# Split weight halves stored with the columns of two k-tiles interleaved

## The chip, the cores and the metric

The kernel runs on one core of one Trainium2 chip. The metric is the device time of one execution, in microseconds. The kernel before takes 2815.72 us, the median of three runs (2814.26 to 2816.58).

## The reference

Two transformer blocks in a row, on one sequence of 256 tokens with 2048 features, all in float32. The first has an adaptive modulation (a matrix of 2048 x 12288 on one vector), a projection `w_in`, stick-breaking attention in 8 heads, sparse attention with an indexer in 8 heads, two output projections with gates, and a feed-forward part of 5632 with a causal convolution of width 3. The second has a projection, 8 heads of attention with a forget gate, 8 heads of a three-branch sparse attention, and a SwiGLU of 5632. Cut to the products that matter here:

```python
def first_block(x, ...):
    mod = silu(c) @ w_ada + b_ada
    h = modulate(rms_norm(x, g_mix), sh1, sc1)
    z = h @ w_in                       # q, k, v, indexer and gates
    ...
    x = x + gt1 * (merged @ w_out)
    h = modulate(rms_norm(x, g_ffn), sh2, sc2)
    a = causal_dwconv(h @ w_gate, conv_w, conv_b)
    return rms_norm(x + gt2 * ((silu(a) * (h @ w_up)) @ w_down), g_final)

def second_block(x, ...):
    x = x + hybrid_mixer(rms_norm(x, attn_norm), w_in, ...)
    return x + (silu(h @ w_gate) * (h @ w_up)) @ w_down   # h = rms_norm(x, ffn_norm)
```

## The kernel before

Nearly all work is products of the activations (256 tokens) with weight matrices that are read once. They are computed to nearly float32 precision with the matmul type fp32r: each operand is written as a high half, rounded to fp32r, plus a low half, the difference; and three products are summed, high x high, high x low and low x high.

A weight tile goes through these steps. SyncE issues a DMA of 512 KB into `raw`, 128 partitions by 1024 words (`load`, L252 to L269): n k-tiles of 128 rows of the matrix, w columns of each, mostly two of 512 or four of 256. `split` (L285 to L305) makes the halves: ScalarE copies `raw` into `wh` in fp32r (L296), VectorE writes the difference into `wl` (L303; GpSimd does the first one, L301). Both have four buffers of [128, 1024] words. `view` (L292) gives both tiles the layout "p (k w)", one k-tile behind the other, so that 128 weight columns are 128 adjacent words of a partition. `products` (L381 to L384) hands out one k-tile after the other.

There are two kinds of groups. In kind "f" the weights are stationary (`mm_f`, L386 to L404): for each 128 columns of the group and each k-tile, the weight columns are loaded and the activations move past them, 256 columns for 256 tokens (258 in the first block's feed-forward part, for the convolution). A group that has `pair` uses the two activation halves at once, since they are adjacent: high weights times 512 columns (L397, or L393 for the first k-tile) and low weights times 256 (L396, or L394). This is called a pair below. The other groups do three matmuls, a triple, L399 to L401:

```python
nc.tensor.matmul(ps, hi[:, fs], xh, start=start, stop=False)
nc.tensor.matmul(ps, hi[:, fs], xl, start=False, stop=False)
nc.tensor.matmul(ps, lo[:, fs], xh, start=False, stop=stop)
```

In kind "t" (`mm_t`, L406 to L417) the activations are stationary and the weights move. These are mostly the products for v, and few. Each matmul comes with a load of its stationary operand, on a queue of its own (PEld in the profile) that runs beside the matmul ahead of it.

The activation halves live in `ring`, 13 slots of [128, 8, n] words: four k-tiles, high and low in turn, with n of 256 or 258.

The order is written out by hand. `run` (L446 to L487) goes over the items; before the matmuls of one item it issues the copies and subtractions of up to three items further on (`AHEAD`, L420; `LAG` holds the subtractions one behind the copies), and `pump_loads` (L423) keeps SyncE up to 10 loads ahead. `spent` counts matmul columns and runs the attention, norm and modulation steps in between, as small pieces on all engines. The change touches only `split` and `products`.

Of the kernel before, what the change touches and what calls it, by code (L numbers as in the profile page):

```python
# [123 lines left out]
def kernel(ctx: ExitStack, tc: tile.TileContext, t):  # L124
# [64 lines left out]
    def psm():  # L189
        return pm.tile([128, 512], F32, name="pm", tag="pm")  # L190
# [37 lines left out]
    def start(gen):  # L228
        active.append(gen)
        return gen  # L230
# [54 lines left out]
    def split(idx, g, ks, off, stage):  # L285

        it, r = items[idx], raw_of[idx]
        k0, n = ks[0], len(ks)
        if it[0] == "w":
            w = g.width  # L290
            src = r[:, k0 - it[2]:k0 - it[2] + n, off:off + w]
            view = lambda x: x[:, :n * w].rearrange("p (k w) -> p k w", w=w)  # L292
            if stage == 0:
                hi = view(wp.tile([128, 1024], F32R, name="wh", tag="wh"))
                half_of[idx, g, k0] = hi
                nc.scalar.activation(out=hi, in_=src, func=AF.Copy)  # L296
            else:
                hi, lo = half_of[idx, g, k0], view(wp.tile([128, 1024], F32R, name="wl", tag="wl"))
                if state["firsts"]:
                    state["firsts"] -= 1  # L300
                    nc.gpsimd.tensor_tensor(out=lo, in0=src, in1=hi.bitcast(F32), op=OP.subtract)  # L301
                else:
                    nc.vector.tensor_sub(out=lo, in0=src, in1=hi.bitcast(F32))  # L303
                half_of[idx, g, k0] = (hi, lo)
            return  # L305
        a = it[1]
        first = a in (0, NKG)
        if stage == 0 and k0 == 0:
            ada_acc[a] = P.get("ft", ab).tile([128, 2, 512], F32, name="adaacc", tag="adaacc", bufs=2)
            if first:  # L310
                ada_ps[a] = psm()
        for k in ks:
            side = k not in FIRST_OWN if first else k % 3 == 1 if a < 2 * NKG else k % 2 == 1
            if side != (stage == 0):
                continue
            own = FIRST_OWN.index(k) if first and not side else k // 2
            acc = ada_acc[a][:, own % 2 if first else int(side), :128 * ADA[a][1]]
            x, cs = r[:, k - it[2], :], cact[:, k:k + 1]
            if side and first:
                for j in range(ADA[a][1]):  # L320
                    nc.tensor.matmul(ada_ps[a][:, j:j + 1], x[:, 128 * j:128 * (j + 1)], cs,
                                     start=(k == 1 and j == 0), stop=False)
            elif own < (2 if first else 1):
                eng = nc.gpsimd if side else nc.vector
                eng.tensor_scalar(out=acc, in0=x, scalar1=cs, scalar2=None, op0=OP.mult)
            elif side:
                nc.scalar.activation(out=x, in_=x, func=AF.Copy, scale=cs)  # L327
                nc.gpsimd.tensor_tensor(out=acc, in0=x, in1=acc, op=OP.add)  # L328
            else:
                nc.vector.scalar_tensor_tensor(out=acc, in0=x, scalar=cs, in1=acc, op0=OP.mult, op1=OP.add)  # L330
        if stage == 1 and ks[-1] == NK - 1:
            if first:
                ada_first(a)
            else:
                fins.append(start(ada_finish(a)))
# [15 lines left out]
    def ada_first(a):  # L351
        acc, ps, w = ada_acc.pop(a), ada_ps[a], 128 * ADA[a][1]
        nc.vector.tensor_add(out=acc[:, 0, :w], in0=acc[:, 0, :w], in1=acc[:, 1, :w])
        for j in range(ADA[a][1]):
            nc.tensor.matmul(ps[:, j:j + 1], acc[:, 0, 128 * j:128 * (j + 1)], ones[:, 0:1], start=False,
                             stop=(j == ADA[a][1] - 1))
        if a == 0:
            h_scale(0)
            ada_put(NKG, ada_ps[NKG], 1)
            ada_put(0, ps, 1)  # L360

    def ada_finish(a):
        acc, w = ada_acc.pop(a), 128 * ADA[a][1]
        s = acc[:, 1, :w]
        yield
        nc.gpsimd.tensor_tensor(out=s, in0=acc[:, 0, :w], in1=s, op=OP.add)
        yield from wait(FW[a // NKG if a < 2 * NKG else 2])
        ps = psm()
        for j in range(ADA[a][1]):
            nc.tensor.matmul(ps[:, j:j + 1], s[:, 128 * j:128 * (j + 1)], ones[:, 0:1], start=True, stop=True)  # L370
        ada_put(a, ps, 1)
# [9 lines left out]
    def products(g, parts):  # L381
        ks = [(half_of[idx, g, ks[0]], kk, k) for idx, ks in parts for kk, k in enumerate(ks)]
        for j, ((hi, lo), kk, k) in enumerate(ks):
            yield hi[:, kk, :], lo[:, kk, :], *g.act(k), g.done == 0 and j == 0, g.done + j + 1 == g.nk  # L384

    def mm_f(g, parts, last):  # L386
        n = g.n
        for f in range(g.width // 128):
            fs = slice(128 * f, 128 * f + 128)
            ps = g.ps[f][:, :n]  # L390
            for hi, lo, xh, xl, both, start, stop in products(g, parts):
                if g.pair and start:
                    nc.tensor.matmul(g.ps[f], hi[:, fs], both, start=True, stop=False)  # L393
                    nc.tensor.matmul(ps, lo[:, fs], xh, start=False, stop=False)  # L394
                elif g.pair:
                    nc.tensor.matmul(ps, lo[:, fs], xh, start=False, stop=False)  # L396
                    nc.tensor.matmul(g.ps[f], hi[:, fs], both, start=False, stop=stop)  # L397
                else:
# [3 lines that stand above are left out]
                spent(3 * n)  # L402
            if last:
                g.evac(f, g.ps[f])  # L404

    def mm_t(g, parts, last):  # L406
        w = g.width
        for b in range(2):
            bs = slice(128 * b, 128 * b + 128)
            ps = g.ps[b][:, :w]  # L410
            for hi, lo, xh, xl, _, start, stop in products(g, parts):
                nc.tensor.matmul(ps, xh[:, bs], hi, start=start, stop=False)  # L412
                nc.tensor.matmul(ps, xh[:, bs], lo, start=False, stop=False)  # L413
                nc.tensor.matmul(ps, xl[:, bs], hi, start=False, stop=stop)  # L414
                spent(3 * w)
            if last:
                g.evac(b, g.ps[b])  # L417
# [12 lines left out]
    def split_stage(stage):  # L430
        idx, g, ks, off = halves[state["split"][stage]]
        if stage == 0:
            pump_loads(idx - 1)
        if items[idx][0] == "call":
            if stage == 1:
                items[idx][1]()
        elif items[idx][0] != "raw":
            split(idx, g, ks, off, stage)
        state["split"][stage] += 1
# [1349 lines left out]
```

## Time and profile before

| | |
|---|---|
| median of the runs | 2815.72 us |
| the profiled execution | 2818.41 us |
| its span | 2816.6 us |
| TensorE busy, matmuls | 2734.5 us, 97% |
| its weight loads | 2496.7 us, 89% |
| VectorE | 2007.7 us, 71% |
| ScalarE | 1424.9 us, 51% |
| GpSimd | 841.1 us, 30% |
| DMA | 590.45 MB, mean 210 GB/s |
| mean granted clock of TensorE | 0.993 |

The span is the time from the first to the last recorded instruction; the execution's own time is 1.8 us longer. PE is TensorE's matmuls, PEld its weight loads, DVE VectorE, ACT ScalarE, POOL GpSimd. Matmuls are pipelined and their ends are modelled, so that one starts while another still counts as busy; the time that one takes is read from the distance between starts, or from a count in a stretch without idle time. PEclk 1.00 means that the clock of 2.4 GHz was granted for the whole stretch. In "128*128 128x512" the first pair is the stationary tile (partitions * columns), the second the moving operand.

### The profile page before, as it was taken

Reading aid. Unit: us, or ns where it says so; the run is one execution under the profiler, and the core shown is the slowest. Engines: PE = TensorE matmul, PEld = TensorE weight load, DVE = VectorE, ACT = ScalarE, POOL = GpSimd, SP = SyncE. Lnnn points to the kernel's source line nnn. Section 1 sums busy time; section 2 is a strip of 40 time slices with the busy share of each in tenths; the row PEclk is TensorE's granted clock in tenths of the full one; section 3 lists DMA queues with packets and bytes.
Section 4 is the critical chain, followed back from the end, with each engine's and each line's share of the span. In section 5 each row is a group of like instructions: output and inputs, shape, how many; then the busy total and the mean of one; then the engine's idle time right before and its main releaser. Section 6 shows DMA issues by size and latency. Waiting matters only on the chain.

```text
span 2816.6 us, 47791 instructions
## 1 busy us (share of the span) xinstructions
PE 2734.5 (97%) x18364; PEld 2496.7 (89%) x18364; DVE 2007.7 (71%) x2804; ACT 1424.9 (51%) x2124; POOL 841.1 (30%) x710
## 2 busy tenths in 40 slices
PE   7899999899999999999999999999999999999999
PEld 7788887788988999989999888989998888888888
DVE  7999997979888986655666765676776665556654
ACT  5555564555556554434454544555554544344443
POOL 3867752545754531000110310211222220012210
PEclk9999999999999999999999999999999999999999
DMA  9777777878887876566666575544566565566654
GB/s 316 250 249 256 241 219 203 268 242 280 291 276 233 287 260 183 184 188 186 180 180 191 183 229 172 163 123 144 186 188 187 180 189 193 187 187 187 187 195 142
DMA packets 334944, 590.45 MB, mean 210 GB/s; under 512 B 21234, under 2 KB 85594, under 8 KB 334716
## 3 DMA queue, kind: packets, MB, share of 16 engines
q1 hardware_dynamic: 331236, 583.61, 65.7%
q10 hardware_dynamic: 3480, 3.79, 0.7%
q8 instruction: 144, 2.36, 0.3%
q14 instruction: 84, 0.69, 0.1%
HBM read 581.49 MB, written 5.78 MB: 209 GB/s over the span
## 4 chain that ended last, share of the span: by engine, by line
PE 76%; DVE 10%; DMA 5%; issue 4%; POOL 3%; ACT 2%; SPq 0%; DVEq 0%; ACTq 0%; POOLq 0%
PE pg L397 25%; PE pg L396 13%; PE pg L399 9%; PE pg L400 9%; PE pg L401 9%; DVE wl L303 4%; DVE adaacc L330 3%; PE pg L393 2%; DMA raw<-in_w_in 2%; PE pm L728 1%; PE pg L412 1%; ACT wh L296 1%; PE pg L414 1%; PE pg L413 1%; DMA raw<-in_w_out 1%
## 5 line engine op out<-in xcount | busy, mean ns | idle before, releaser
L303 DVE TENSOR_TENSOR wl<-raw,wh 128x1024 fp32r<-128x1024 f32 (+1 forms) x921 | 1192.1, 1306 | 658.3 <-ACT wh L296 656.1
L296 ACT ACTIVATE wh<-raw 128x1024 fp32r<-128x1024 f32 (+2 forms) x922 | 934.2, 1026 | 883.2 <-PE pg L397 497.6
L397 PE MATMUL pg<-ring,wh 128*128 128x512 f32 x3384 | 1203.9, 396 | 0.0
L396 PE MATMUL pg<-ring,wl 128*128 128x256 f32 x3384 | 957.9, 283 | 7.6 <-DVE wl L303 7.6
L399 PE MATMUL pg<-ring,wh 128*128 128x256 f32 (+1 forms) x2828 | 813.7, 288 | 9.8 <-DVE ring L1093 3.6
L401 PE MATMUL pg<-ring,wl 128*128 128x256 f32 (+1 forms) x2828 | 799.9, 283 | 13.9 <-DVE wl L303 13.8
L400 PE MATMUL pg<-ring,wh 128*128 128x256 f32 (+1 forms) x2828 | 803.7, 284 | 0.0
L397 PEld LDWEIGHTS pg<-ring,wh 128*128 128x128 f32 x3384 | 638.2, 189 | 141.4
L396 PEld LDWEIGHTS pg<-ring,wl 128*128 128x128 f32 x3384 | 638.4, 189 | 23.6 <-DVE wl L303 9.5
L401 PEld LDWEIGHTS pg<-ring,wl 128*128 128x128 f32 x2828 | 541.4, 191 | 17.8 <-DVE wl L303 17.8
L399 PEld LDWEIGHTS pg<-ring,wh 128*128 128x128 f32 x2828 | 538.2, 190 | 19.7 <-issue 7.6
L400 PEld LDWEIGHTS pg<-ring,wh 128*128 128x128 f32 x2828 | 539.5, 191 | 3.6 <-issue 2.2
L531 POOL TENSOR_TENSOR ring<-gy,ring 128x256 fp32r<-128x256 f32 x88 | 107.1, 1230 | 661.9 <-ACT ring L529 661.9
L328 POOL TENSOR_TENSOR adaacc<-raw,adaacc 128x512 f32<-128x512 f32 (+2 forms) x152 | 230.6, 1517 | 247.4 <-ACT raw L327 197.4
L330 DVE SCALAR_TENSOR_TENSOR adaacc<-raw,cact,adaacc 128x512 f32<-128x512 f32 (+2 forms) x228 | 234.2, 1031 | 3.6 <-DMA raw<-in_w_ada 2.0
L1268 POOL TENSOR_TENSOR gy<-ga,rb 128x256 f32<-128x256 f32 x44 | 53.6, 1228 | 331.1 <-ACT ga L203 331.1
L516 POOL TENSOR_TENSOR ring<-pt,ring 128x256 f32<-128x256 f32 x95 | 109.7, 1167 | 50.5 <-ACT pt L515 50.3
L327 ACT ACTIVATE raw<-raw,cact 128x512 f32<-128x512 f32 (+2 forms) x152 | 103.1, 681 | 23.3 <-DMA raw<-in_w_ada 16.9
L1163 POOL TENSOR_TENSOR ssq<-ssq,sq 128x256 f32<-128x256 f32 x60 | 63.8, 1075 | 145.3 <-ACT sq L1161 144.0
L1406 POOL TENSOR_TENSOR hm<-hm,hsq 128x512 f32<-128x512 f32 (+1 forms) x15 | 18.4, 1224 | 286.3 <-ACT hsq L203 286.3
L393 PE MATMUL pg<-ring,wh 128*128 128x512 f32 x200 | 81.9, 410 | 7.0 <-DVE ring L1169 3.6
L412 PE MATMUL pg<-wh,ring 128*128 128x512 f32 (+3 forms) x236 | 84.2, 357 | 0.0
(300 smaller groups left out, 2665.1 us busy)
## 6 DMA issues: line engine op xcount, KB each, us to landing
raw<-in_w_in SPq DMA_DIRECT2D x240, 512.0 KB, 4.6
raw<-in_w_gate SPq DMA_DIRECT2D x176, 512.0 KB, 4.2
raw<-in_w_up SPq DMA_DIRECT2D x176, 512.0 KB, 4.4
raw<-in_w_down SPq DMA_DIRECT2D x176, 512.0 KB, 4.2
raw<-in_w_ada SPq DMA_DIRECT2D x144, 512.0 KB, 5.4
raw<-in_w_out SPq DMA_DIRECT2D x64, 512.0 KB, 4.6
raw<-in_w_ada SPq DMA_DIRECT2D x64, 384.0 KB, 4.1
raw<-in_w_o_sb SPq DMA_DIRECT2D x16, 512.0 KB, 5.1
```

Source lines behind the costliest of these rows:

```text
L296: nc.scalar.activation(out=hi, in_=src, func=AF.Copy)
L303: nc.vector.tensor_sub(out=lo, in0=src, in1=hi.bitcast(F32))
L328: nc.gpsimd.tensor_tensor(out=acc, in0=x, in1=acc, op=OP.add)
L330: nc.vector.scalar_tensor_tensor(out=acc, in0=x, scalar=cs, in1=acc, op0=OP.mult, op1=OP.add)
L393: nc.tensor.matmul(g.ps[f], hi[:, fs], both, start=True, stop=False)
L396: nc.tensor.matmul(ps, lo[:, fs], xh, start=False, stop=False)
L397: nc.tensor.matmul(g.ps[f], hi[:, fs], both, start=False, stop=stop)
L399: nc.tensor.matmul(ps, hi[:, fs], xh, start=start, stop=False)
L400: nc.tensor.matmul(ps, hi[:, fs], xl, start=False, stop=False)
L401: nc.tensor.matmul(ps, lo[:, fs], xh, start=False, stop=stop)
L412: nc.tensor.matmul(ps, xh[:, bs], hi, start=start, stop=False)
L516: nc.gpsimd.tensor_tensor(out=y, in0=x, in1=y, op=OP.add)
```

## The change

In groups of kind "f" the halves are stored with the columns of two k-tiles in turn: word 2j + b of a block is column j of k-tile b of the two. A stationary tile, 128 columns of one k-tile, is then every other word of 256 adjacent ones, 8 bytes from column to column. An item with a single k-tile leaves the other places of the block empty. ScalarE's copy writes with that step, VectorE's subtraction reads the high half and writes the low half with it, and `products` hands out the tiles with it. `raw`, the DMAs, the activations, the groups of kind "t", the instructions and their order stay as they are.

```diff
@@ -290,6 +290,10 @@
             w = g.width
             src = r[:, k0 - it[2]:k0 - it[2] + n, off:off + w]
             view = lambda x: x[:, :n * w].rearrange("p (k w) -> p k w", w=w)
+            if g.kind == "f":
+
+                view = lambda x: x[:, :max(n, 2) * w].rearrange("p (a w b) -> p a b w", w=w, b=2)[:, :, :min(n, 2), :]
+                src = src.rearrange("p (a b) w -> p a b w", b=min(n, 2))
             if stage == 0:
                 hi = view(wp.tile([128, 1024], F32R, name="wh", tag="wh"))
                 half_of[idx, g, k0] = hi
@@ -381,7 +385,8 @@
     def products(g, parts):
         ks = [(half_of[idx, g, ks[0]], kk, k) for idx, ks in parts for kk, k in enumerate(ks)]
         for j, ((hi, lo), kk, k) in enumerate(ks):
-            yield hi[:, kk, :], lo[:, kk, :], *g.act(k), g.done == 0 and j == 0, g.done + j + 1 == g.nk
+            hi, lo = ((x[:, kk // 2, kk % 2, :] if g.kind == "f" else x[:, kk, :]) for x in (hi, lo))
+            yield hi, lo, *g.act(k), g.done == 0 and j == 0, g.done + j + 1 == g.nk
```

## Rows read from the trace of the kernel before

**Rows 1.** The chain of waits: shares by engine, then by line.

```profile
PE 76%; DVE 10%; DMA 5%; issue 4%; POOL 3%; ACT 2%; SPq 0%; DVEq 0%; ACTq 0%; POOLq 0%
...
PE pg L397 25%; PE pg L396 13%; PE pg L399 9%; PE pg L400 9%; PE pg L401 9%; DVE wl L303 4%; DVE adaacc L330 3%; PE pg L393 2%; DMA raw<-in_w_in 2%; PE pm L728 1%; PE pg L412 1%; ACT wh L296 1%; PE pg L414 1%; PE pg L413 1%; DMA raw<-in_w_out 1%
```

**Rows 2.** Busy time by stretch: window, us, each engine's us (x instructions), PEclk, DMA share, GB/s.

```profile
0.00:420.00 420.00, 377.94 (x2594) 349.27 (x2595) 377.63 (x534) 234.86 (x424) 270.07 (x231) 0.98 0.80 255
...
420.00:860.00 440.00, 410.40 (x2530) 360.58 (x2528) 368.98 (x510) 235.24 (x349) 232.81 (x164) 0.97 0.81 259
...
860.00:1500.00 640.00, 637.86 (x4915) 618.07 (x4915) 442.74 (x597) 323.92 (x426) 121.06 (x133) 1.00 0.67 208
...
2060.00:2816.00 756.00, 753.07 (x4307) 657.44 (x4306) 444.17 (x521) 344.05 (x455) 116.05 (x95) 1.00 0.59 184
```

**Rows 3.** By stretch, one line of matmuls each: L396, L393, L399; PE (x), PEld (x).

```profile
2104.00:2804.00 700.00, 527.81 (x1878) 353.18 (x1878) 1.00 0.59 186
...
2104.00:2804.00 700.00, 44.19 (x112) 21.08 (x112) 1.00 0.59 186
...
1300.00:1480.00 180.00, 140.98 (x500) 94.00 (x500) 1.00 0.61 180
```

**Rows 4.** Timeline of TensorE: start us, duration us, instruction; two stretches.

```profile
1740.65 0.28 PE L399 MATMUL pg<-ring,wh 128*128 128x256 f32 x1
...
1745.75 0.28 PE L399 MATMUL pg<-ring,wh 128*128 128x256 f32 x1
...
2046.61 0.29 PE L399 MATMUL pg<-ring,wh 128*128 128x256 f32 x1
...
2052.01 0.28 PE L399 MATMUL pg<-ring,wh 128*128 128x256 f32 x1
```

**Rows 5.** Weight loads by source line: duration ns min/median/max, first and last start, forms.

```profile
L763 PEld LDWEIGHTS pm<-t,relb x2: 81/82/84, 452.9 to 453.0; 32*8 32x8 f32 x2
...
L728 PEld LDWEIGHTS pm<-pcT,vcT x32: 181/182/184, 1839.6 to 1940.7; 32*128 32x128 f32 x32
...
L1500 PEld LDWEIGHTS pm<-ringw,ring x64: 134/136/156, 1669.1 to 1709.5; 128*34 128x34 f32 x64
...
L399 PEld LDWEIGHTS pg<-ring,wh x2828: 186/188/335, 30.7 to 2069.0; 128*128 128x128 f32 x189
```

**Rows 6.** Instructions ahead of and behind 860 us: L396, L393, L399; then one form.

```profile
0.00:860.00 860.00, 199.56 (x687) 131.06 (x687) 0.98 0.80 257
...
860.00:2816.00 1956.00, 758.37 (x2698) 507.31 (x2698) 1.00 0.61 189
...
0.00:860.00 860.00, 21.93 (x48) 9.89 (x48) 0.98 0.80 257
...
860.00:2816.00 1956.00, 59.99 (x152) 28.64 (x152) 1.00 0.61 189
...
0.00:860.00 860.00, 264.93 (x912) 178.06 (x912) 0.98 0.80 257
...
860.00:2816.00 1956.00, 623.09 (x2176) 409.99 (x2176) 1.00 0.61 189
...
L399 PE MATMUL pg<-ring,wh 128*128 128x258 f32 x1408 | 398.4, 283 | 1.1 <-DVE ga L1231 1.0
```

**Rows 7.** VectorE's groups by line and form: xcount, busy us, mean ns, idle before.

```profile
L303 DVE TENSOR_TENSOR wl<-raw,wh 128x1024 fp32r<-128x1024 f32 x853 | 1130.3, 1336 | 639.8 <-ACT wh L296 637.7
...
L303 DVE TENSOR_TENSOR wl<-raw,wh 128x512 fp32r<-128x512 f32 x56 | 51.6, 922 | 0.4 <-ACT wh L296 0.2
...
L1472 DVE TENSOR_SCALAR gat<-gat 128x24 f32<-128x24 f32 x2 | 0.4, 180 | 0.7 <-ACT gat L203 0.7
...
L1382 DVE TENSOR_SCALAR gcol<-vec 128x1 f32<-128x1 f32 x6 | 0.4, 138 | 0.0
```

**Rows 8.** VectorE at L303 alone, by stretch.

```profile
0.00:420.00 420.00, 179.73 (x145) 0.98 0.80 255
...
420.00:860.00 440.00, 184.04 (x124) 0.97 0.81 259
```

## Prediction

> **What bounds the kernel now.** I read the chain of waits first: three quarters of it is TensorE, and of the lines on it the five of the two matmul forms hold some 65 of 100 [rows 1]. The stretches say where: behind 860 us TensorE is idle for 2 us in 640 and for 3 in 756, while VectorE has 197 and 312 us free there; ahead of 860 us TensorE, VectorE (378 of 420, 369 of 440) and the transfers (0.80) are all nearly full, and none of them alone sets the pace [rows 2]. So up to 860 us TensorE's time counts in part, behind it in full.
>
> Then the pace, since the matmuls overlap and their own durations (283 ns for 256 columns) say little. Two stretches without an idle moment give it. From 2104 to 2804 us there are 1878 + 112 pairs (one matmul of 512 columns and one of 256): 700 us / 1990 = 351.8 ns for a pair. From 1300 to 1480 us there are 500 triples (three of 258 columns): 180 us / 500 = 360 ns [rows 3]. The granted clock in both is 1.00, the level of 2.4 GHz, at which the 768 columns of a pair take 320 ns and the 774 of a triple 322.5. So 32 to 38 ns of each are lost, and nothing that the waits name ends them.
>
> What they are shows where the same instruction with the same shapes runs at two paces. At 1740 us 45 matmuls of 256 columns start in 5.10 us, 113.3 ns apart; at 2046 us 45 of them take 5.40 us, 120.0 ns apart [rows 4]. Engines, lines and tile names are the same; what differs is the ring slot that the moving operand is read from, and a slot of 8 x 258 words is 32 x 256 + 64 bytes, so that each slot lies 64 bytes further against the weight tiles (4096 bytes each) in a period of 256. I read it as the two reads of TensorE, the moving columns and the next stationary tile, getting into each other's way or not, by how their addresses lie. Reading 256 moving columns at 2.4 GHz goes through memory at 9.6 bytes a ns. A stationary column takes (182 - 82) / (128 - 8) = 0.83 ns by the loads of 128 and of 8 columns on 32 partitions [rows 5], so a load of adjacent words goes at 4.8 bytes a ns: the faster read overtakes it and meets it again and again.
>
> **The change part by part.** No instruction is added, removed or moved; no wait, DMA or queue changes. What changes is the addresses of three things.
>
> (1) The stationary loads of the "f" groups. These are two in each pair and three in each triple: 2850 pairs and 2176 triples behind 860 us, 735 and 912 ahead of it; 1408 of the triples have 258 columns, and all of these lie behind [rows 6]. In the "t" groups the weights are the moving operand and stay as they were. A load now steps 8 bytes a column, 9.6 bytes a ns: as fast as the moving read. Two reads of one speed that are apart stay apart, and two that meet are pushed apart once. I take it that a load then costs what it costs in the good stretch: 340 ns for a triple of 256 columns (3 x 113.3), 343 with 258 (two more columns each at about 0.45). The 258-column triples then gain 17 ns each: 1408 x 17 = 24 us. Those of 256 columns stand between 340 and 360 by their slot, 350 on a mean that I estimate as the middle: 768 x 10 = 8 us. For pairs no good stretch is at hand; a load gains 5.7 ns in the one form and 3.3 in the other, so I take 5 and two loads: 2850 x 10 = 28 us. Sum behind 860 us: 60. Ahead of it (735 + 912) x 10 = 16 us, of which I count half, since VectorE and the transfers are as full: 8. Together 68 us.
>
> Bounds of this part. At best nothing of a load is left: 31.8 ns a pair, 37.5 and 30 a triple, (2850 x 31.8 + 1408 x 37.5 + 768 x 30) / 1000 = 166, and half of (735 x 31.8 + 912 x 30) / 1000 = 51: 192 us, or 2624. At worst the load itself gets slower with a step. The one stepped load in the trace has 34 columns 16 words apart: 136 ns, where 34 adjacent ones would take 82 + 26 x 0.83 + 6 (the 6 from 188 against 182 ns for 128 partitions and 32) = 110, so 26 / 34 = 0.8 ns a column more [rows 5]. With that, the 128 columns of a load, 107 ns now, take 209; a triple waits for three of them, 627 ns instead of some 355, and a pair for two, 418 instead of 352: 3088 x 272 + 3585 x 66 ns = 1080 us, about 3900. A step of 2 words is far nearer to the adjacent loads than to 16 words, so I take no slower load. [...]
>
> (2) The writes of the high halves on ScalarE and of the low halves on VectorE, and (3) VectorE's read of the high half, step 8 bytes as well. A word of the subtraction costs (1336 - 922) / 512 = 0.81 ns now. The only stepped operation of VectorE at hand has 24 words in 180 ns where one word takes 138, which is 1.8 ns a word and mostly overhead, I believe [rows 7]. From both sides: nothing, or 1.0 ns x 1024 = 1.0 us for each subtraction. [...] What hides a small rise is VectorE's free time, 42 us in the first stretch with 145 subtractions (0.29 us each) and 71 us in the second with 124 [rows 2, 8]; ScalarE has more to spare in both.
>
> The profiled execution took 2818.4 us, its span 2816.6; the median of the runs is 2815.7, inside 0.1%. Less 68 us: 2750 from the profiled one, 2748 from the median, which I give.
>
> **The rivals.**
>
> No change. The 113.3 and 120.0 could come from how the moving read alone lies in memory, and a load as such cost nothing. For it: the loss grows with the columns, 32 ns for two loads and 33 to 38 for three. Against it: the good stretch. The layout then does nothing of what counts: 2816. [...]
>
> Loads get in the way more often. A load of adjacent words takes two words out of each 8 bytes; the stepped one touches twice as many places in its 107 ns. If the touches count and not how the reads keep step (as they would if a load runs from the last column to the first, against the moving read), each load costs its present price once more: the same 68 us on the other side, 2884. For it: the loss is there in nearly every slot, as with chance meetings. It decides from a pair of more than 352 ns in the last stretch.
>
> VectorE becomes the bound. If a stepped subtraction takes 0.5 us more, the first stretch needs 378 + 73 = 451 us of its 420 and the end is 31 us later, 2847; with 1.0 us it is 103 us there and 53 in the second, 2972. It decides from 0.29 us. [...]
>
> Slower loads, to 3900 us at most, as in (1).
>
> **How the numbers follow.** The forecast has a chance of 0.46, with a range of its own of 2690 to 2800. No change 0.21, more meetings 0.20, VectorE 0.09, slower loads 0.04. About 0.2% (6 us) is what a measurement of this kernel can tell from none; so faster 0.46, same 0.21, slower 0.33. The range 2680 to 2890 holds nearly all of the forecast, the case of no change, more than half of the third and the mild end of the fourth, 0.8 in all.
>
> **What would show it.** Right: in the last stretch a pair at 342 ns or less, a triple of 258 columns near 343, the two paces of [rows 4] alike in all slots, loads still 188 ns, the low half still 1336 ns. No change: the same 351.8 and 360. Wrong on the other side: pairs above 352 with loads of 188 ns (more meetings), loads above 195 ns (a slower load), or low halves above 1600 ns with TensorE idle behind VectorE ahead of 860 us. That the two reads hinder each other at all would be wrong if triples from different slots still differ by 7 ns and pairs don't move.

## The result: slower by 0.8%

The changed kernel takes 2837.18 us (median of 4 runs, 2836.03 to 2839.91), the kernel before 2814.99 (2813.00 to 2816.58); the ratio is 1.0081, 95% interval 1.0063 to 1.0098. That is 22 us more, where 68 less were forecast. Its profiled execution took 2839.9 us, the span 2838.1. The instructions and their order on TensorE are the same, 18364 matmuls, so that each can be set beside its own of before.

The profile after, in the order in which the rows of before stand. First the chain of waits, by engine and by line:

```profile
PE 79%; DVE 8%; issue 4%; DMA 4%; POOL 3%; ACT 2%; SPq 0%; DVEq 0%; ACTq 0%; POOLq 0%
PE pg L402 24%; PE pg L401 12%; PE pg L404 10%; PE pg L405 10%; PE pg L406 10%; DVE wl L307 4%; DVE adaacc L334 2%; DMA raw<-in_w_in 2%; PE pg L398 1%; ACT wh L300 1%; PE pg L417 1%; PE pg L418 1%; PE pg L419 1%; PE pm L733 1%; PE pg L399 1%
```

TensorE holds more of it than before (79 against 76 of 100 [rows 1]), and no new wait stands on it. The same four stretches as [rows 2] (window, us, then each engine's busy us and instructions, PEclk, DMA share, GB/s):

```profile
0.00:420.00 420.00, 380.14 (x2588) 353.28 (x2589) 378.45 (x533) 242.00 (x423) 265.29 (x230) 0.96 0.80 255
420.00:860.00 440.00, 409.64 (x2505) 363.68 (x2504) 369.32 (x508) 244.33 (x349) 233.14 (x164) 0.97 0.80 257
860.00:1500.00 640.00, 638.70 (x4860) 621.69 (x4859) 439.13 (x587) 340.17 (x419) 119.04 (x133) 1.00 0.67 207
...
2060.00:2816.00 756.00, 756.00 (x4352) 677.36 (x4352) 446.79 (x529) 371.16 (x470) 120.77 (x100) 1.00 0.60 188
```

From 860 to 1500 us TensorE is as busy as before and gets through 4860 matmuls instead of 4915: it is slower, not idle. The steady stretches, shifted with the work, as in [rows 3] (L401 and L398 are the pairs, L404 the triples):

```profile
2124.00:2824.00 700.00, 524.43 (x1869) 367.09 (x1869) 1.00 0.59 186
...
2124.00:2824.00 700.00, 44.01 (x112) 22.10 (x112) 1.00 0.59 186
...
1309.00:1489.00 180.00, 140.58 (x495) 97.11 (x494) 1.00 0.60 179
```

A pair takes 700 / 1981 = 353.4 ns (351.8 before), a triple of 258 columns 180 / 495 = 363.6 (360). And the two stretches of 45 matmuls that stood at 113.3 and 120.0 ns [rows 4]:

```profile
1754.73 0.28 PE L404 MATMUL pg<-ring,wh 128*128 128x256 f32 x1
...
1760.13 0.28 PE L404 MATMUL pg<-ring,wh 128*128 128x256 f32 x1
...
2064.39 0.28 PE L404 MATMUL pg<-ring,wh 128*128 128x256 f32 x1
...
2069.79 0.29 PE L404 MATMUL pg<-ring,wh 128*128 128x256 f32 x1
```

Both now take 5.40 us. The paces did become alike, as forecast, but at the bad value: the good one is gone. The loads and the writers of the halves, beside [rows 5, 7] (loads: min/median/max ns; writers: busy us, mean ns); ScalarE's copy of before stands last:

```profile
L404 PEld LDWEIGHTS pg<-ring,wh x2828: 192/196/333, 29.3 to 2087.0; 128*128 128x128 f32 x189
...
L307 DVE TENSOR_TENSOR wl<-raw,wh 128x1024 fp32r<-128x1024 f32 x853 | 1130.1, 1336 | 657.4 <-ACT wh L300 648.0 <-DMA raw<-in_w_out 3.4 <-DMA raw<-in_w_down 3.2
...
L300 ACT ACTIVATE wh<-raw 128x1024 fp32r<-128x1024 f32 x854 | 968.4, 1146 | 821.8 <-PE pg L402 443.1 <-PE pg L405 216.8 <-issue 55.8
...
L296 ACT ACTIVATE wh<-raw 128x1024 fp32r<-128x1024 f32 x854 | 892.9, 1056 | 858.8 <-PE pg L397 497.6 <-PE pg L400 225.5 <-DMA raw<-in_w_in 43.1
```

A load's median goes from 188 to 196 ns, the subtraction stays at 1336, ScalarE's copy goes from 1056 to 1146.

Where the 22 us are: for each matmul I took the distance from its start to the next one's, in both traces, and subtracted. Distances under 330 ns, which leave hardly room for a wait, sum to 21.4 us more; the longer ones, which hold the waits, to 0.4 more. The first matmul behind 860 us starts 4.9 us later now, so 5 of the 22 us come ahead of it and 17 behind. The granted clock is not the cause: ahead of 860 us it was at 0.5 for 61 us in this trace and for 41 in that of before (256 columns start 213 ns apart there and 512 columns 427, in both traces: 1.2 columns a ns, and so 2.4, or 2.4 GHz, at 1.00), but behind 860 us it was 1.00 in both, and of the 5 us ahead, short distances at 2.4 GHz in both traces make 4.1.

### The profile page after: what moved, and what is told of

The parts are those of the page before. It is cut to its first block, busy times and chain, and to the rows that moved or that the text cites. A ratio compares the mean times of both kernels' runs of the same rounds, so it can differ in the third digit from the quotient of the medians.

```text
span 2838.1 us, 47791 instructions
## 1 busy us (share of the span) xinstructions
PE 2757.9 (97%) x18364; PEld 2545.5 (90%) x18364; DVE 2007.9 (71%) x2804; ACT 1494.5 (53%) x2124; POOL 832.1 (29%) x710
## 4 chain that ended last, share of the span: by engine, by line
PE 79%; DVE 8%; issue 4%; DMA 4%; POOL 3%; ACT 2%; SPq 0%; DVEq 0%; ACTq 0%; POOLq 0%
PE pg L402 24%; PE pg L401 12%; PE pg L404 10%; PE pg L405 10%; PE pg L406 10%; DVE wl L307 4%; DVE adaacc L334 2%; DMA raw<-in_w_in 2%; PE pg L398 1%; ACT wh L300 1%; PE pg L417 1%; PE pg L418 1%; PE pg L419 1%; PE pm L733 1%; PE pg L399 1%
## 5 line engine op out<-in xcount | busy, mean ns | idle before, releaser
L300 ACT ACTIVATE wh<-raw 128x1024 fp32r<-128x1024 f32 (+2 forms) x922 | 1011.4, 1112 | 846.6 <-PE pg L402 443.1
L401 PE MATMUL pg<-ring,wl 128*128 128x256 f32 x3384 | 959.1, 283 | 7.6 <-DVE wl L307 7.5
L404 PE MATMUL pg<-ring,wh 128*128 128x256 f32 (+1 forms) x2828 | 820.0, 290 | 12.8 <-DVE ring L1098 4.4
L402 PEld LDWEIGHTS pg<-ring,wh 128*128 128x128 f32 x3384 | 667.1, 197 | 121.7
L401 PEld LDWEIGHTS pg<-ring,wl 128*128 128x128 f32 x3384 | 668.4, 198 | 21.5 <-DVE wl L307 9.1
L404 PEld LDWEIGHTS pg<-ring,wh 128*128 128x128 f32 x2828 | 558.6, 198 | 22.2 <-issue 7.1
L406 PEld LDWEIGHTS pg<-ring,wl 128*128 128x128 f32 x2828 | 560.9, 198 | 15.0 <-DVE wl L307 14.8
L405 PEld LDWEIGHTS pg<-ring,wh 128*128 128x128 f32 x2828 | 559.7, 198 | 3.3 <-issue 2.1
L334 DVE SCALAR_TENSOR_TENSOR adaacc<-raw,cact,adaacc 128x512 f32<-128x512 f32 (+2 forms) x228 | 232.4, 1024 | 3.4 <-DMA raw<-in_w_ada 1.8
L1411 POOL TENSOR_TENSOR hm<-hm,hsq 128x512 f32<-128x512 f32 (+1 forms) x15 | 18.4, 1226 | 293.3 <-ACT hsq L203 293.3
L398 PE MATMUL pg<-ring,wh 128*128 128x512 f32 x200 | 81.5, 407 | 6.1 <-DVE ring L1174 3.4
```

## The experiments

Four things were to be told apart: the price of a stepped load, the place of the weight tiles against the moving operand, ScalarE's longer copy, and which half does it.

**Scratch data, one step at a time** (`e1_bench`). The core of the kernel, run for each step, shift and number of columns:

```python
for i in range(48):
    st = cut(w, 1024 * (i % 4), 128, step)
    m = cut(x, sh + 512 * (i % 6), n, mstep)
    nc.tensor.matmul(acc[i % 4][:, :n], st, m, start=True, stop=True)
```

> Only matmuls and copies on scratch data, none of the reference's work. TensorE runs stretches of 48 matmuls back to back (fp32r, stationary 128 columns, weights and moving operand in two tiles whose starts are equal modulo 256 bytes), with the stationary columns 1, 2, 4 or 8 words apart, the moving operand 256 or 512 columns, adjacent, and shifted by 0, 64, 128 or 192 bytes; then 8 moving columns (the load alone), one moving column repeated 256 times, moving columns 2 words apart, and moving columns in reverse order. Theory 1, the two reads of TensorE hinder each other: 256 columns (106.7 ns at 2.4 GHz) take 113 to 120 ns with step 1 depending on the shift, some 2 ns more with step 2, more again with 4 and 8; with one repeated moving column the excess over 106.7 is gone or the same at every step. Theory 2, the load has a price of its own by its step: 8 moving columns take longer with step 2 than with step 1 by the 9 ns that the load's duration rose (189 to 198 ns), and the 256-column pace does not depend on the shift. ScalarE's copy of 1024 words: with step 2 some 90 ns more also while TensorE is idle, if the step itself costs; only beside TensorE, if it is contention.

The timeline of TensorE (start us, length us of the whole row, x matmuls), with 256 moving columns: step 1 at the shifts 0 and 192 bytes, step 2 at the same two, step 4 at 0. The length less the last matmul's own 0.28 us (0.39 in the last row), over x - 1, is the pace.

```profile
53.84 5.08 PE L74 MATMUL acc<-x,w 128*128 128x256 f32 x41
...
71.60 4.92 PE L74 MATMUL acc<-x,w 128*128 128x256 f32 x42
...
77.29 5.08 PE L74 MATMUL acc<-x,w 128*128 128x256 f32 x41
...
95.34 5.08 PE L74 MATMUL acc<-x,w 128*128 128x256 f32 x41
...
102.03 9.49 PE L74 MATMUL acc<-x,w 128*128 128x256 f32 x40
```

By the starts: 120.0, 117.8, 118.6 and 113.3 ns with step 1 at the four shifts, which are the kernel's two paces and what lies between them, without any other engine at work; 120.0 to 121.7 with step 2 at all shifts; 233.3 with step 4, where I had expected a few ns. Moving columns in reverse gave 117.8 to 120.1 with either step. With 512 moving columns the step shows less: 226.7 to 233.3 ns with step 1 at the four shifts, 230.0 to 233.3 with step 2. The writers, each by the mean ns of a copy or subtraction of 1024 words with steps 1, 2 and 4 (ScalarE) and 2 and 4 (VectorE), while TensorE had not begun:

```profile
L56 ACT ACTIVATE sa<-raw 128x1024 fp32r<-128x1024 f32 x4 | 4.2, 1057 | 0.1
...
L56 ACT ACTIVATE sa<-raw 128x1024 fp32r<-128x1024 f32 x4 | 4.6, 1156 | 0.1
...
L56 ACT ACTIVATE sa<-raw 128x1024 fp32r<-128x1024 f32 x4 | 8.2, 2040 | 0.1
...
L59 DVE TENSOR_TENSOR sd<-raw 128x1024 fp32r<-128x1024 f32 x4 | 4.9, 1226 | 0.1
...
L59 DVE TENSOR_TENSOR sd<-raw 128x1024 fp32r<-128x1024 f32 x4 | 8.0, 2010 | 0.1
```

So ScalarE's 90 ns are the step's own price and no contention; VectorE pays nothing for step 2 (1226 ns with step 1, too). Nor do the writers slow TensorE: 600 matmuls with step 1, and 600 with step 2 behind them, took 120.0 ns each, with the copies and subtractions beside them and, at the end, without. The rows with 8 moving columns fell into a stretch with a granted clock of 0.5 to 0.8 and are not used; they were taken again below.

**High halves alone, low halves alone.** The other half keeps its layout; here the edit that leaves the low one plain:

```diff
-                hi, lo = half_of[idx, g, k0], view(wp.tile([128, 1024], F32R, name="wl", tag="wl"))
+                hi, lo = half_of[idx, g, k0], plain(wp.tile([128, 1024], F32R, name="wl", tag="wl"))
...
-            hi, lo = ((x[:, kk // 2, kk % 2, :] if g.kind == "f" else x[:, kk, :]) for x in (hi, lo))
+            hi, lo = hi[:, kk // 2, kk % 2, :] if g.kind == "f" else hi[:, kk, :], lo[:, kk, :]
```

> Only the high halves are stored with two k-tiles in turn, the low halves as before. Theory 1, each load of every other word delays the matmul it runs beside: the high halves are loaded beside the 256-column matmuls of a pair (0.4 ns less each in the changed kernel) and beside two of the three matmuls of a triple (2.0 and 2.5 ns more with 256 columns, 2.0 and 1.5 with 258), so 2828 x 4 = 11 us less 1.5: 2825. Theory 2, ScalarE's copy with a step (1146 instead of 1056 ns) gets into TensorE's way: the whole 22 us, 2837, since only ScalarE's copy writes the high halves.

> Only the low halves are stored with two k-tiles in turn. Theory 1: the low halves are loaded beside the 512-column matmul of a pair (3.0 ns more in the changed kernel, 3384 x 3.0 = 10 us) and beside the second matmul of a triple (1.8 and 0.5 ns more, 4 us): 2829. Theory 2: nothing, 2815, since ScalarE writes as before.

High halves alone: 2825.4 us, ratio 1.0036 (1.0024 to 1.0049). Low halves alone: 2813.99, ratio 1.0000 (0.9991 to 1.0009). Theory 2, ScalarE's copy as the whole cause, falls: with the slow copy in it (1141 ns), the first costs 11 us, not 22. Theory 1 gave the first and missed the second by 15 us: the two don't add up to 22. The paces (table below) say why: with either half alone the pairs get faster, and only with both slower.

**Every fourth word** (`e4_step4`). The 128-column blocks of a k-tile stored in turn (`products` and `mm_f`, left out here, cut the tiles to match):

```diff
+            if g.kind == "f":
+                view = lambda x: x[:, :n * w].rearrange("p (k c f) -> p k f c", k=n, c=128)
+                src = src.rearrange("p k (f c) -> p k f c", c=128)
...
```

> The columns of the 128-column blocks of one k-tile stored in turn instead of two k-tiles: a stationary tile of a group of 512 columns is every fourth word, of 256 every other, of 128 adjacent. Theory 1, what counts is how many places a load touches: more again than with every other word, a second 22 us or more on top, 2855 to 2900, with pairs above 356 ns. Theory 2, the price is ScalarE's copy alone: it goes as that copy's duration, near 2837 if it stays at 1146 ns.

4243.37 us, ratio 1.5081 (1.506 to 1.510), far beyond either. The loads of the triples' first matmul:

```profile
L402 PEld LDWEIGHTS pg<-ring,wh x2828: 187/330/341, 30.7 to 3240.4; 128*128 128x128 f32 x189
```

330 ns instead of 188, and the pace is the load's: most pairs take about 473 ns and most triples about 700, two and three times the 233.3 of the scratch data with step 4. "How many places a load touches" has the direction, but the price is no small one per meeting: a load has a rate of its own.

**Scratch data again: the load alone, fewer columns, the kernel's own sequences** (`e5_bench2`).

> Only matmuls on scratch data again, none of the reference's work. (a) 512 and 256 moving columns beside loads of 128, 96, 64 and 32 stationary columns: theory 1 (the reads hinder each other) expects the excess over columns / 2.4 (13 to 20 ns for 512) to fall with the columns loaded, to a few ns at 32; if it stays, the excess is the moving operand's own. (b) 512 columns from one repeated moving column: theory 1 expects 213 ns plus a few with step 1 and 2. (c) 8 moving columns at the full clock, the load alone: 112 ns with step 1, 118 with step 2, 233 with step 4, as the repeated moving column showed; if step 2 costs nothing there, the load has no price of its own. Step 3 lies at 112 to 120 if the step costs by words, near 175 if by places of 16 bytes. (d) The kernel's own sequences, pairs (256 columns on low, 512 on high weights) and triples, on one data layout, with both tiles at 0, 64, 128 or 192 bytes against the moving operand: if the cause lies in these addresses and steps alone, pairs with both steps 2 come out at 350 to 358 ns and 3 ns above those with step 1 on a mean of the four places, triples 4 to 6 ns above, and with one of the steps 2 the 512-column matmul shows no rise; if not, the rise of the kernel comes from what runs beside it (ScalarE's and VectorE's accesses). Among the 16 places of high and low weights with step 1, one should give pairs under 345 ns (226.7 + 113.3 = 340 if the best of the two single rows can be had together).

The kernel's sequences, with `hi` and `lo` cut with step 1 or, as the change does, 2:

```python
for f in range(4):
    for k in range(4):
        xh, xl, both = (x[:, 512 * k + p:512 * k + q] for p, q in ((0, 256), (256, 512), (0, 512)))
        if kind == "pair":
            mm(f, 256, lo(f, k), xh)
            mm(f, 512, hi(f, k), both)
        else:
            mm(f, 256, hi(f, k), xh)
            mm(f, 256, hi(f, k), xl)
            mm(f, 256, lo(f, k), xh)
```

Timeline rows: one moving column repeated 256 times beside loads of step 1 and 2; 512 columns beside loads of 32 stationary columns; 512 times one column; pairs with both tiles 192 bytes off, steps 1 and 2; triples with both 64 bytes off, steps 1 and 2.

```profile
123.75 3.96 PE L64 MATMUL acc<-x,w 128*128 128x256 f32 x34
...
128.47 4.05 PE L64 MATMUL acc<-x,w 128*128 128x256 f32 x33
...
73.00 7.58 PE L64 MATMUL acc<-x,w 128*32 128x512 f32 x32
...
97.01 7.29 PE L64 MATMUL acc<-x,w 128*128 128x512 f32 x33
...
338.00 10.29 PE L64 MATMUL acc<-x,w 128*128 128x512 f32 x57
...
384.12 10.47 PE L64 MATMUL acc<-x,w 128*128 128x512 f32 x57
...
544.76 10.25 PE L64 MATMUL acc<-x,w 128*128 128x256 f32 x89
...
682.91 10.85 PE L64 MATMUL acc<-x,w 128*128 128x256 f32 x89
```

By the starts: (c) a load alone takes 111.7 ns with step 1, 117.8 with step 2, 173.3 with step 3 and 233.3 with step 4, the same beside 8 moving columns as beside a repeated one (step 3 was run only with 256). Steps 2, 3 and 4 touch 64, 96 and 128 places of 16 bytes: 1.84, 1.81 and 1.82 ns for each. Step 8 touches 128 as well, and took 237.8 ns beside a repeated column in the first scratch run; that it costs hardly more than step 4 is what speaks for 16 bytes. Step 1 touches 32, which would be 58 ns; on this reading another limit, 0.87 ns a column, decides there, and at step 2 the places have just overtaken the columns, by 6 ns. The writers: VectorE pays nothing for step 2 (1226 ns) and 64% for step 4 (2010 ns); at step 2 TensorE's loads take 5% more and ScalarE's copies 9% (1156 ns against 1057).

(a) Theory 1, by which the excess falls with the columns loaded, does not hold. 512 columns take 226.7 ns beside loads of 128 columns, 230.1, 230.0 and 231.6 beside 96, 64 and 32. The excess over 213 (512 columns at 2.4 a ns) does not shrink with what is loaded. With 256 columns the pace was 120.0, 113.4 and 117.7 ns beside 128, 64 and 32, never near 106.7. (b) With a repeated column the excess shrinks to 2.5 ns (215.8), with step 1 and 2 alike. So the excess belongs to reading many different columns, and how they lie to the weights picks its size (226.7 to 233.3 ns at the four shifts of the first scratch run).

(d) The kernel's rise is there without any other engine: pairs with equal places have a mean of 351.1 ns with steps 1 and 355.1 with steps 2, and only 350.1 and 349.2 with one half stepped; triples 352.3, 360.8, 357.5 and 357.7. And place by itself, with adjacent words, moves pairs between 340.0 and 353.3.

**Moving the low halves by some bytes** (`e6_pad64`, `e7_pad_ring`, `e9_gap128`, `e10_gap64`). All loads of adjacent words, as before; only a gap:

```diff
+    gap = ctx.enter_context(tc.tile_pool(name="gap", bufs=1))
+    wq = ctx.enter_context(tc.tile_pool(name="wq", bufs=4))
...
+    gap.tile([128, 48], F32, name="gap")
...
-                hi, lo = half_of[idx, g, k0], view(wp.tile([128, 1024], F32R, name="wl", tag="wl"))
+                hi, lo = half_of[idx, g, k0], view(wq.tile([128, 1024], F32R, name="wl", tag="wl"))
```

> The kernel before, with 192 unused bytes between the buffers of the high and of the low halves, so that the high ones lie 64 bytes further than the low ones modulo 256; nothing else is changed, all loads read adjacent words. If the place of the two weight tiles against the moving operand sets the pace, as the scratch-data rows say (pairs 346.7, 353.3, 351.3, 353.2 ns at equal places, 351.3, 340.0, 346.8, 346.7 with this shift), the kernel's 3584 pairs cost 18 us less and its 1680 triples of 256 columns 3 us more: 14 us faster, some 2801, less what is hidden ahead of 860 us. If not, 2815.

2804.22 us, ratio 0.9958 (0.9945 to 0.9972): place moves the pace, and 10 of the 14 us came.

> As the run with 192 bytes between the halves, and every other ring slot's 256-column halves start 64 bytes later, in space that the slot has anyway, so that only two of the four places occur: half of the pairs at 340.0 and half at 346.7 ns, triples of 256 columns at 353.4 and 346.6. By the rows on scratch data that is 29 us less than before: 2786, less what is hidden ahead of 860 us, some 2786 to 2793. If place is not what counts, 2815.

```diff
-        return ring.tile([128, 8, n], dt, name="ring", tag="ring")
...
+        a = 16 * (BUF[made[0] - 1] % 2)
+        whole = ring.tile([128, 8 * T + 16], dt, name="ring", tag="ring")
+        return whole[:, a:a + 8 * T].rearrange("p (j n) -> p j n", n=T)
```

(BUF lists which of the 13 slots each tile gets.)

2810.48 us, ratio 0.9984 (0.9975 to 0.9993): 4 us of 29, a miss. The place that took 340.0 ns on scratch data (high halves 64 bytes further than the moving operand modulo 256, low ones level with it) stands at 352.5 in the kernel. Why this row doesn't carry over isn't settled; in the kernel the slot, and with it the place, changes every four k-tiles.

> The kernel before with 128 unused bytes between the buffers of the high and of the low halves (192 in the run before this), all loads of adjacent words. By the rows on scratch data with the kernel's own counts of places: 4 us less than before, 2811. If only the equal places of before are bad in the kernel's own sequence, whatever the distance, it is near 2804 as with 192 bytes.

With `gap.tile([128, 32], ...)`, and 16 for the next one:

2814.66 us, ratio 0.9995 (0.9986 to 1.0004): no gain, so not just any distance helps.

> The same with 64 bytes between the buffers. By the rows on scratch data: 12 us less than before, 2803. In the kernel with 192 bytes the place that scratch data had at 340.0 ns stood at 352.7, so such a row may again not carry over; 704 pairs at 353 instead of 340 would leave 3 us less than before, 2812.

2798.98 us, ratio 0.9942 (0.9929 to 0.9954): the fastest of all, 15.7 us under the kernel before. The steady pairs (L399, then L396):

```profile
2095.00:2785.00 690.00, 525.13 (x1879) 354.38 (x1880) 1.00 0.60 189
...
2095.00:2785.00 690.00, 44.08 (x112) 21.08 (x112) 1.00 0.60 189
```

690 / 1991 = 346.6 ns instead of 351.8, with the same loads and no other edit. Sorted by place (high halves 0, 64, 128 and 192 bytes further than the moving operand, low ones 64 more), this kernel's pairs take 346.8, 351.3, 347.1 and 341.0 ns where scratch data had 346.6, 350.0, 346.7 and 340.0: these four rows do carry over.

**Both steps 2 at all places, and on the changed kernel** (`e8_bench3`, `e11_change_gap128`).

The loop is that of the second scratch run, with `hi` and `lo` cut with step 2, and `x[:, 516 * k + p:516 * k + p + 258]` for 258 columns.

> Matmuls on scratch data, none of the reference's work: pairs and triples with both steps 2 at all 16 places of the two tiles, and triples of 258 columns in rows of 258 words, with steps 1 and 2 at equal places. If every other word costs by the load's own length (118 instead of 112 ns), no triple falls below 353 ns at any place (with step 1 the best were 340), and pairs have a best place near 347; if it was only bad places, some reach 340 as before. The 258-column triples: near 360 ns with step 1, some 4 ns more with step 2, as in the kernels.

The best of the 16 places, for pairs and for triples:

```profile
136.16 9.87 PE L52 MATMUL acc<-x,w 128*128 128x512 f32 x56
...
251.31 10.86 PE L52 MATMUL acc<-x,w 128*128 128x256 f32 x90
```

Pairs lie between 346.7 and 360.0 ns, triples between 356.6 and 364.8: no triple gets back to 340, as the load's length demands (3 x 117.8 = 353). On a mean over all 16 places pairs take 352.4 ns, where step 1 had 348.2, and triples 360.3, where it had 353.1. For pairs the step costs 4 ns at equal places, 6 where the halves lie 64 or 192 bytes apart, and 0.7 where they lie 128 apart. 258 columns: 361.5 on a mean with step 1, 365.9 with step 2.

> The changed kernel (both halves every other word) with 128 unused bytes between the buffers of the high and of the low halves. If the rise of its pairs (353.9 against 351.6 ns) comes from the places at which two stepped tiles stand against the moving operand, it goes: by the rows on scratch data with both steps 2, 16 us less in pairs and 3 in triples of 256 columns, 2819. If the rise is a price of the step itself, it stays at 2837. The triples stay some 6 ns above those of before in either case, since their load alone takes 118 ns instead of 112, so that it does not come below 2815 + 12.

The gap of 128 bytes, as a tile of 32 words in the changed kernel: 2824.77 us, ratio to the kernel before 1.0036 (1.0023 to 1.0048), 12 us under the changed kernel. The steady pairs (L404, then L401) take 698 / 1991 = 350.6 ns:

```profile
2115.00:2813.00 698.00, 527.18 (x1879) 367.72 (x1879) 1.00 0.59 187
...
2115.00:2813.00 698.00, 43.98 (x112) 22.07 (x112) 1.00 0.59 187
```

**All kernels side by side.** The mean pace of pairs and triples, from all starts in each trace without a wait (under 430 ns for the whole), times the counts 3584, 1680 and 1408, against the measured difference to before:

| kernel | pair ns | triple, 256 | triple, 258 | sum of the differences, us | measured, us |
|---|---|---|---|---|---|
| before | 351.6 | 353.3 | 360.5 | | |
| changed | 353.9 | 360.8 | 364.8 | 8 + 13 + 6 = +27 | +22 |
| high halves alone | 350.6 | 357.9 | 363.1 | -4 + 8 + 4 = +8 | +11 |
| low halves alone | 349.7 | 357.9 | 362.1 | -7 + 8 + 2 = +3 | 0 |
| gap of 192 bytes | 348.8 | 353.7 | 361.2 | -10 + 1 + 1 = -8 | -10 |
| the same, two places | 350.0 | 351.8 | 361.3 | -6 - 3 + 1 = -7 | -4 |
| gap of 128 bytes | 351.3 | 351.9 | 362.0 | -1 - 2 + 2 = -1 | 0 |
| gap of 64 bytes | 346.8 | 354.0 | 360.9 | -17 + 1 + 1 = -16 | -16 |
| changed, gap of 128 bytes | 351.4 | 359.7 | 365.4 | -1 + 11 + 7 = +17 | +10 |

Three numbers a kernel account for all of them to within 7 us; the sums are of paces before rounding. They leave out that a slower pace ahead of 860 us counts only in part.

## Why the prediction was wrong

*What bounds the kernel* held. TensorE's pace moved the time, no wait did. Of the loss ahead of 860 us some 8.5 us can be priced (735 pairs at 2.3 ns, 912 triples at 7.5) and 5 show in the end: "half of it" was near.

*The step that failed* is in part (1): "a load then costs what it costs in the good stretch", 340 ns for a triple. Two things were wrong in it. First, the load of every other word is longer by itself, 117.8 ns instead of 111.7. With 256 moving columns (106.7 ns at 2.4 a ns) the load is the longer of the two, so that three of them set a floor of 353 for a triple (the lowest of the scratch places had 356.6); it went to 360.8, 7.5 ns up instead of 10 down. That is 13 of the table's 27 us, with 6 more from 258 columns. Sorted by the place of the tiles against the moving operand, triples of 256 columns took 346.8 ns at one of the four places before and 353.2 to 359.6 at the others, so the mean was 353.3 and not the middle of 350; now they take 359.3 to 361.8 at all of them. The floor shows why there was nothing to gain. How the mean comes to stand 7.5 ns above it is measured but not explained: one stepped load in three (the low halves) and two in three cost 4.6 ns alike.

Second, the picture of a fast read that overtakes a slow one and meets it again fell in the second scratch run: the excess stays when a quarter of the columns is loaded. The pairs' 10 ns of gain had no other ground. They rose by 2.3, and how much a pair rises hangs on place: with both tiles 0, 64, 128 and 192 bytes further than the moving operand, pairs went from 353.0, 352.9, 351.0 and 349.4 ns to 352.6, 351.3, 354.9 and 357.5. With 128 bytes between the halves stepped pairs take 351.4, plain ones 351.3, and the changed kernel is 12 us faster. It is not place alone: over the 16 places of scratch data the step costs a pair 4 ns on a mean.

*The bound for a slower load* was looked at and then given 0.04. I had the row for it (34 columns 16 words apart, 0.8 ns a column more [rows 5]) and went by the nearest row, adjacent words, since 2 is nearer to 1 than to 16. The price is no line between them: 0.05 ns a column at step 2, 0.95 at step 4. Nor was the upper end one; every fourth word cost more than 16 words were priced at (4243 us against 3900).

*Parts (2) and (3)*: of the two prices named for a subtraction, nothing and 1.0 us, the forecast has nothing, my estimate, which no row of before shows. It was right for VectorE, 1336 ns. ScalarE's 90 ns I had not priced; its cover, the free half of ScalarE, hides it: the waits grew by 0.4 us.

*The rivals.* "Loads get in the way more often" named the side and its mark, a pair above 352 ns, with the loads above the 195 ns that were the mark of "slower loads". Its mechanism, twice the meetings for twice the places, is not what the runs show, and its 68 us were three times too many. "VectorE becomes the bound" and "no change" fell. That a load as such costs nothing, as "no change" had it, is half borne out: the amount loaded beside 512 columns does not matter (226.7 to 231.6 ns from 128 columns down to 32), the place does (pairs 340.0 to 353.3 ns).

What stays open: what in the memory makes a pair take 340 ns at one place and 353 at another, and why two stepped halves at equal places cost pairs 4 ns and one costs none. Both were reproduced on scratch data, neither was explained.

## What to carry to other kernels

Before giving an operand a step, time its load alone with that step: when the matmul is no longer than the load (here 106.7 ns beside 111.7), a few ns of load can be a few ns of the matmuls (here 6.1 more of each load and 7.5 of a triple). When matmuls of one shape run at two paces, move the buffers against each other by 64 or 128 bytes first; it costs a few bytes, and here 64 bytes gave 16 us where a new layout lost 22. Rows from a loop at one fixed place rank such moves only roughly (14 us forecast and 10 measured, 29 and 4, 4 and 0, 12 and 16), so try them in the kernel.

## What was not expected of the hardware

- A load of 128 fp32r columns: 111.7, 117.8, 173.3 and 233.3 ns with steps of 1, 2, 3 and 4 words; 1.8 ns for each 16 bytes touched from step 2 to step 4. ScalarE: 1057, 1156 and 2040 ns for 1024 words written with steps 1, 2 and 4; VectorE: 1226, 1226, 2010.
- 256 moving columns two words apart, beside weights of adjacent words: 230.0 ns instead of 120.0.
- Loops of pairs or triples at a fixed place mostly settle at 340.0, 346.7, 353.3 or 360.0 ns, 6.67 ns apart, the time of 16 columns at 2.4 GHz; 22 of the 32 loops with step 1 lie within 0.2 ns of one of these.
